# Opening of a hybrid encoder kernel: all 512 tokens taken channels-first, and the row norm applied to V, dt and K at their eviction

## The chip, the cores and the metric

The kernel runs on one core of a Trainium2 chip. The metric is the device time of one execution in microseconds (us); the kernel before is given as the median of three executions. Profiles are of one execution each, and positions such as "at 25.54" are microseconds from the start of its span.

## What is computed

One encoder layer on 512 tokens of 1024 channels. The part that the change touches is the first norm and the projections that read it:

```python
h = rmsnorm(x, pre_mix_norm[l])            # x * rsqrt(mean(x*x) + 1e-6) * g
proj = h @ w_in[l]                         # all projections in one matrix
z, xbc, dt_raw, q, k, v, gates = split_cols(proj, IN_SPLITS)
y_ssd  = ssd_branch(z, xbc, dt_raw, ...)   # bidirectional Mamba-2 scan
y_attn = window_attention(q, k, v, ...) @ w_attn_out[l]
...                                        # gates, output projection, norm, squared-ReLU MLP, norm
```

The norm's factor r = rsqrt(mean(x*x) + eps) is one number per token. A product of h with a weight may therefore be made from x*g without r, and r multiplied in afterwards.

## The kernel before, in words

**Arithmetic.** Nearly every product is made of three passes in the type fp32r: an operand a is split into a high part (a cast to fp32r, on ScalarE) and a low part (a minus the high part, on VectorE or GpSimd), and `mm3` (L456) adds high*high, high*low and low*high in PSUM. A product in plain fp32 needs no split, but shows in the trace as two matmul records, each slower per column.

**Quanta and order.** The program is a list of quanta, each a product with its weight chunks. A chunk is loaded into one of three raw buffers (`wr`), cast into `wh` by ScalarE and subtracted into `wl` by GpSimd in four pieces (L525, L529). Actions such as evictions are hung on a quantum number with `at`; a fraction such as 2.5 means the middle of quantum 2. After everything has been emitted, a planner (`Planner.plan`, called by `chain`, L549) orders the instructions of each engine by its own costs and fixes that order with dependencies. PSUM has eight banks: three of the tag `pp` (projections) and five of the tag `ps`, each handed out in a ring.

**The opening.** Eight warm-up products on a tile of ones (L682) come first. Then V (256 columns) and dt (64 columns) are made with tokens on the partitions, 320 columns at a time, contraction in eight pieces k of 128 channels:

- Tokens 0 to 255 arrive channels-first from the host (`in_xt`, tiles `xt`, five pieces `X_CHUNKS`). They are multiplied by the norm's gain g into `xg` (L697, L699), and the products `ps<-wr,xg` are plain fp32, 2 token blocks x 8 k (L643). r is put in at the eviction (L629, L630).
- All 512 tokens arrive a second time as token rows (`in_x`, tiles `x`, L715, eight loads of 256 KB), to get the mean squares (L723 on ScalarE, L724 on VectorE, L726 and L727 on GpSimd). For tokens 256 to 511 the rows are scaled by r (L760, L761), transposed on TensorE (L763, `tr` at L454, 16 of them) and split into `h` (L475, L476); their V and dt products are three-pass, 2 blocks x 8 k x 3 (L655).
- For tokens 0 to 255, r is spread over the partitions by `scale_tokens` (L730): a diagonal matrix `dg` times ones, in fp32, into a `pp` bank; `xg` times that gives `hf` (L743), which is split into the other half of `h` (L745, L746).
- `h` is complete before the first K product. The two K quanta (L896) follow, 24 matmuls of 512 columns each, and are split from PSUM straight into `KH` and `KL` (L888 to L891); then two Q quanta (L915, L916), the scores of attention head 0 (`ps<-KH,Q` and `ps<-KL,Q`), and the x quanta of the scan. `dt_math` (L813) computes dt and its running sums from the dt rows on the way.

## Time and profile before

| | |
|---|---|
| median of 3 executions | 1074.58 us (1074.38 to 1079.08) |
| the profiled execution's own time | 1074.73 us |
| its span in the profile | 1072.9 us |
| TensorE busy | 1062.9 us, 99% of the span |
| VectorE, ScalarE, GpSimd busy | 758.4, 656.8, 796.5 us |
| moved by DMA | 133.20 MB |

The profile's page lists, for each engine, busy time, the chain of work that ended last, and groups of equal instructions; a row of the timeline gives start, length, engine, line, operation, output<-inputs, shape and count, and in brackets how long the engine had been idle before and what released it. PE is TensorE's matmuls, PEld its weight loads, DVE VectorE, ACT ScalarE, POOL GpSimd, SP the queue that issues most loads. Lengths of matmul records overlap, so a pace is read from starts, not from lengths.

### The profile page before, as it was taken

Reading aid. Unit: us, or ns where it says so; the run is one execution under the profiler, and the core shown is the slowest. Engines: PE = TensorE matmul, PEld = TensorE weight load, DVE = VectorE, ACT = ScalarE, POOL = GpSimd, SP = SyncE. Lnnn points to the kernel's source line nnn. Section 1 sums busy time; section 2 is a strip of 40 time slices with the busy share of each in tenths; the row PEclk is TensorE's granted clock in tenths of the full one; section 3 lists DMA queues with packets and bytes.
Section 4 is the critical chain, followed back from the end, with each engine's and each line's share of the span. In section 5 each row is a group of like instructions: output and inputs, shape, how many; then the busy total and the mean of one; then the engine's idle time right before and its main releaser. Section 6 shows DMA issues by size and latency. Waiting matters only on the chain.

```text
span 1072.9 us, 16653 instructions
## 1 busy us (share of the span) xinstructions
PE 1062.9 (99%) x5542; PEld 894.7 (83%) x5542; DVE 758.4 (71%) x1363; ACT 656.8 (61%) x1409; POOL 796.5 (74%) x993
## 2 busy tenths in 40 slices
PE   9999999999999999999999999999999999999997
PEld 7888888888888888888888888889888888888885
DVE  5577778787885878787976536698663574574588
ACT  6766877676686867676777424466555444444552
POOL 5756458567677699899989966215587897898994
PEclk9999999999999999999999999999999999999999
DMA  8342324433443426244535544317211421424222
GB/s 287 117 129 89 123 79 121 146 102 103 130 119 108 154 99 182 87 136 142 165 109 153 177 150 145 112 59 262 89 68 67 152 97 60 157 93 150 73 99 78
DMA packets 61509, 133.20 MB, mean 124 GB/s; under 512 B 9064, under 2 KB 18920, under 8 KB 61424
## 3 DMA queue, kind: packets, MB, share of 16 engines
q1 hardware_dynamic: 61136, 131.76, 38.6%
q8 instruction: 43, 0.70, 0.3%
q10 hardware_dynamic: 288, 0.39, 0.1%
q14 instruction: 42, 0.34, 0.1%
HBM read 127.63 MB, written 4.49 MB: 123 GB/s over the span
## 4 chain that ended last, share of the span: by engine, by line
PE 97%; DVE 1%; DMA 1%; ACT 0%; issue 0%; POOL 0%; SPq 0%; DVEq 0%; POOLq 0%
PE pp L450 62%; PE ps L450 32%; PE ps L454 3%; DMA wr<-in_wv 1%; PE pp L454 0%; DVE x L1419 0%; DVE acc L1398 0%; SPq L690 0%; DVE wl L620 0%; DVEq L1783 0%; DVE ag L1698 0%; DVE h L1406 0%; POOLq L1783 0%; ACT wh L617 0%; POOL mrs L1412 0%
## 5 line engine op out<-in xcount | busy, mean ns | idle before, releaser
L529 POOL TENSOR_TENSOR wl<-wr,wh 128x256 fp32r<-128x256 f32 (+1 forms) x519 | 415.9, 831 | 166.5 <-ACT wh L525 163.2
L450 PE MATMUL pp<-h,wh 128*128 128x512 f32 (+1 forms) x1728 | 524.5, 385 | 0.0
L450 PEld LDWEIGHTS pp<-h,wh 128*128 128x128 f32 x1728 | 318.5, 188 | 61.6 <-issue 0.5
L450 PE MATMUL pp<-h,wl 128*128 128x512 f32 (+1 forms) x864 | 333.9, 386 | 0.0
L525 ACT CAST wh<-wr 128x1024 fp32r<-128x1024 f32 (+1 forms) x130 | 135.3, 1041 | 127.5 <-PE pp L450 99.4
L450 PEld LDWEIGHTS pp<-h,wl 128*128 128x128 f32 x864 | 162.4, 188 | 32.0 <-POOL wl L529 0.2
L1624 POOL TENSOR_TENSOR wl<-wd,wh 128x256 fp32r<-128x256 f32 x158 | 131.6, 871 | 11.8 <-ACT wh L1621 11.8
L1621 ACT CAST wh<-wd 128x512 fp32r<-128x512 f32 x92 | 53.2, 618 | 38.4 <-PE ps L450 21.6
L450 PE MATMUL ps<-wl,fh 128*128 128x512 f32 x184 | 71.7, 390 | 0.0
L450 PE MATMUL ps<-wh,fl 128*128 128x512 f32 x184 | 71.6, 389 | 0.0
L450 PE MATMUL ps<-wh,fh 128*128 128x512 f32 x184 | 71.6, 389 | 0.0
L1459 DVE SCALAR_TENSOR_TENSOR pp<-pp,r 128x256 f32<-128x256 f32 (+1 forms) x31 | 17.3, 559 | 65.5 <-ACT r L1456 65.4
L1183 ACT ACTIVATE n<-cb,tables 128x128 f32<-128x128 f32 x128 | 47.6, 392 | 16.0 <-DVE cb L1174 12.3
L1017 DVE SCALAR_TENSOR_TENSOR u<-pp,cv,u 128x510 f32<-128x510 f32 (+1 forms) x64 | 47.7, 746 | 10.1 <-ACT u L1013 8.8
L1222 POOL TENSOR_TENSOR w<-w,E 128x256 f32<-128x256 f32 x48 | 40.5, 858 | 16.2 <-DVE w L1218 15.2
L1184 ACT ACTIVATE m<-cb,tables 128x128 f32<-128x128 f32 x128 | 47.6, 390 | 7.2 <-DVE cb L1174 6.5
L1115 POOL TENSOR_TENSOR xd<-x,tables 128x256 f32<-128x256 f32 x48 | 32.4, 693 | 17.4 <-ACT x L1040 15.0
L1179 ACT ACTIVATE rf<-rf,tables 128x128 f32<-128x128 f32 x128 | 42.4, 392 | 4.1 <-DMA rf<-csT 4.1
L1177 POOL TENSOR_TENSOR rb<-rb,tables 128x512 f32<-128x512 f32 x32 | 36.6, 1147 | 9.9 <-DMA rb<-csT 7.9
L949 ACT ACTIVATE P<-P,mx 128x384 f32<-128x384 f32 (+1 forms) x64 | 35.2, 551 | 14.1 <-DVE mx L946 14.1
L1676 DVE TENSOR_TENSOR acc<-acc,ps 128x512 f32<-128x512 f32 x46 | 31.3, 680 | 15.8 <-PE ps L450 15.6
L1185 DVE TENSOR_TENSOR m<-m,n 128x512 f32<-128x512 f32 x32 | 29.5, 922 | 16.6 <-ACT m L1184 16.5
(291 smaller groups left out, 2202.7 us busy)
## 6 DMA issues: line engine op xcount, KB each, us to landing
wr<-in_w_in_b SPq DMA_DIRECT2D x74, 512.0 KB, 3.7
wr<-in_w_mlp_in_b SPq DMA_DIRECT2D x32, 512.0 KB, 3.5
wd<-in_w_mlp_out SPq DMA_DIRECT2D x64, 256.0 KB, 4.8
rb<-csT SPq DMA_DIRECT2D x32, 256.0 KB, 4.0
rf<-csT SPq DMA_DIRECT2D x32, 256.0 KB, 3.7
wr<-in_w_ssd_out_b SPq DMA_DIRECT2D x13, 512.0 KB, 3.4
x<-in_x SPq DMA_DIRECT2D x16, 256.0 KB, 4.7
E<-csE SPq DMA_DIRECT2D x32, 128.0 KB, 4.3
```

Source lines behind the costliest of these rows:

```text
L450: self.nc.tensor.matmul(out, lhsT, rhs, start=start, stop=stop, skip_group_check=more)
L525: self.nc.scalar.copy(hi[:, :m], raw)
L529: engines[e].tensor_tensor(lo[:, c], raw[:, c], hi[:, c].bitcast(F32), op=ALU.subtract)
L949: nc.scalar.activation(p[:, :w], p[:, :w], AF.Exp, bias=mx[:, n:n + 1], accum_out=sm[:, n:n + 1])
L1017: nc.vector.scalar_tensor_tensor(u[:, a:e], ps[:, a + d:e + d], self.wtap(t, b), u[:, a:e], op0=ALU.mult, op1=ALU.add)
L1177: nc.gpsimd.tensor_tensor(v4(rb), v4(rb), cs[:, 1].unsqueeze(2).to_broadcast([128, 4, 128]), op=ALU.subtract)
L1179: nc.scalar.activation(v4(rf)[:, h], v4(rf)[:, h], AF.Identity, bias=ncs[:, 0, h:h + 1])
L1183: nc.scalar.activation(v4(n)[:, h], cb[:, 0], AF.Copy, scale=dt[:, 0, h:h + 1])
L1184: nc.scalar.activation(v4(m)[:, h], cb[:, 1], AF.Copy, scale=dt[:, 1, h:h + 1])
L1222: nc.gpsimd.tensor_tensor(wc, wc, E[:, d], op=ALU.add)
L1621: nc.scalar.copy(hi, src)
L1624: (nc.vector if q == 512 else nc.gpsimd).tensor_tensor(lo[:, c], src[:, c], hi[:, c].bitcast(F32), op=ALU.subtract)
```

## The change

All eight channel pieces of all 512 tokens are now loaded channels-first, as eight tiles `xt` of 128x512; no token rows are loaded and nothing is transposed. Each `xt` is multiplied by g and split into a new pair `hr` ("raw h", without r) by ScalarE and VectorE. V, dt and K are made from `hr`: V and dt with four token blocks and three passes, except k = 0, which stays plain fp32 (`PLAIN = 1`); r is multiplied in when V and dt are evicted, and K is multiplied by r spread over the partitions (`rb`) when it is evicted, into a new tile `kf`, which is then split. The mean squares come from the `xt` tiles: ScalarE squares them, VectorE adds them into an even and an odd tile, and eight TensorE products with a single column of ones (`token_sums`) sum over the channels. One GpSimd power gives all four columns of r. `scale_tokens` now handles four token blocks, and makes `h` from `xt` for all 512 tokens, while K is already being computed. The planner's constants for early loads change too.

The core of the diff:

```diff
-X_CHUNKS = ((0, 1), (1, 3), (3, 5), (5, 7), (7, 8))
+W_CHUNKS = ((0, 1), (1, 2), (2, 5), (5, 8))
+PLAIN, SUMS_AT, SCALE_AT = 1, 2.5, 3.5
-RATE, EARLY, LAND = 260, 350, 2500
+RATE, EARLY, START, LAND = 260, 370, 20000, 2500
...
         def done(t, ps):
-            bias = self.row[:, :64]
-            if t < 2:
-                r = self.rst0[:, t:t + 1]
-                nc.scalar.activation(self.V[0][:, t], ps[:, :256], AF.Copy, scale=r)
-                nc.vector.scalar_tensor_tensor(self.dtv[:, t], ps[:, 256:320], r, bias, op0=ALU.mult, op1=ALU.add)
-            else:
-                nc.scalar.copy(self.V[1][:, t - 2], ps[:, :256])
-                nc.vector.tensor_tensor(self.dtv[:, t], ps[:, 256:320], bias, op=ALU.add)
...
+            bias, r = self.row[:, :64], self.rst0[:, t:t + 1]
+            nc.scalar.activation(self.V[t // 2][:, t % 2], ps[:, :256], AF.Copy, scale=r)
+            nc.vector.scalar_tensor_tensor(self.dtv[:, t], ps[:, 256:320], r, bias, op0=ALU.mult, op1=ALU.add)
...
+                for k in range(k0, k1):
+                    for t in range(4):
+                        ps = banks[t][:, :320]
+                        if k < PLAIN:
+                            self.mm(ps, self.xg[k][:, tok(t)], raw[:, k - k0], k == 0, k == 7)
+                        else:
+                            hi, lo = self.hr[k]
+                            self.mm3(ps, (hi[:, tok(t)], lo[:, tok(t)]), (wh[:, k - k0], wl[:, k - k0]), k == 0, k == 7)
...
+    def raw_tokens(self):
+        nc = self.nc
+        for k, x in enumerate(self.xt):
+            g = self.gT[:, k:k + 1]
...
+            hi, lo = self.hr[k]
+            self.split_by(hi, lo, x, g)
+        self.token_scales()
+
+    def token_scales(self):
...
+        even, odd = get("sq"), get("sq")
+        for k, x in enumerate(self.xt):
+            to = (even, odd)[k % 2]
+            if k < 2:
+                nc.scalar.activation(to, x, AF.Square, scale=D ** -0.5)
+            else:
+                sq = self.bank("pp")
+                nc.scalar.activation(sq, x, AF.Square, scale=D ** -0.5)
+                nc.vector.tensor_tensor(to, to, sq, op=ALU.add)
+        self.squares = even, odd
+
+    def token_sums(self, ones):
...
+        ps = self.bank("pp")
+        for t in range(4):
+            for sq in (even, odd):
+                self.mm(ps[:, t:t + 1], sq[:, t * 128:(t + 1) * 128], ones[:, :1], sq is even, sq is odd)
+        self.slots.put(even, odd)
+        nc.vector.tensor_scalar(self.rst0, ps[:, :4], EPS, None, op0=ALU.add)
+        nc.gpsimd.tensor_tensor(self.rst0, self.rst0, self.mhalf[:, 0:1].to_broadcast([128, 4]), op=ALU.pow)
...
         rb = self.bank("pp")
-        for t in range(2):
+        for t in range(4):
             dg = get("dg", (128, 128))
-            nc.gpsimd.tensor_scalar(dg, self.ident, self.rst0[:, t:t + 1], None, op0=ALU.mult)
+            nc.vector.tensor_scalar(dg, self.ident, self.rst0[:, t:t + 1], None, op0=ALU.mult)
             self.mm(rb[:, t * 128:(t + 1) * 128], ones, dg, True, True)
...
+        self.rb = get("rb")
+        nc.scalar.copy(self.rb, rb)
         for k in range(8):
-            x = hf[k // 2][:, k % 2 * 256:(k % 2 + 1) * 256]
-            nc.vector.tensor_tensor(x, rb[:, :256], self.xg[k], op=ALU.mult)
...
+            x = self.xt[k]
+            hi, lo = self.h[k]
+            nc.vector.scalar_tensor_tensor(x, x, self.gT[:, k:k + 1], rb, op0=ALU.mult, op1=ALU.mult)
             nc.scalar.copy(hi, x)
-            nc.gpsimd.tensor_tensor(lo, x, hi.bitcast(F32), op=ALU.subtract)
...
+            for e, c in ((nc.vector, slice(0, 512)),) if k % 2 else ((nc.gpsimd, slice(0, 256)), (nc.gpsimd, slice(256, 512))):
+                e.tensor_tensor(lo[:, c], x[:, c], hi[:, c].bitcast(F32), op=ALU.subtract)
...
         def k_done(ps):
+            x = get("kf")
+            nc.vector.tensor_tensor(x, ps, self.rb, op=ALU.mult)
...
-                nc.scalar.copy(KH[a], ps[a])
-                nc.vector.tensor_tensor(KL[a], ps[a], KH[a].bitcast(F32), op=ALU.subtract)
-                nc.scalar.copy(KH[b], ps[a])
+                nc.scalar.copy(KH[a], x[a])
+                nc.vector.tensor_tensor(KL[a], x[a], KH[a].bitcast(F32), op=ALU.subtract)
+                nc.scalar.copy(KH[b], x[a])
...
-        hh = lambda: self.h
+        hh = lambda: self.hr
         return [self.cm(self.d_w_in_b, C_K - 64 + 128 * i, hh, k_done) for i in range(2)]
```

What the planner makes of it, at three places. First TensorE, where the V and dt products end and K begins. Before, the last token block's last pass (bank ps_299, weights from k = 7) is followed at once by the first K matmul (pp_408):

```order
L450 MATMUL ps_299<-wh_170,h_105 128x320
L450 MATMUL ps_299<-wl_171,h_105 128x320
L450 MATMUL ps_299<-wh_170,h_106 128x320
L450 MATMUL pp_408<-h_91,wh_314 128x512
L450 MATMUL pp_408<-h_92,wh_314 128x512
```

Now the eight one-column sums stand between (pp_325; sq_188 is the even, sq_189 the odd tile of squares; one pair of the four is shown), and K (pp_382) reads `hr`:

```order
L452 MATMUL ps_213<-wh_161,hr_120 128x320
L452 MATMUL ps_213<-wl_162,hr_120 128x320
L452 MATMUL ps_213<-wh_161,hr_121 128x320
L452 MATMUL pp_325<-ones_79,sq_188 128x1
L452 MATMUL pp_325<-ones_79,sq_189 128x1
L452 MATMUL pp_382<-hr_106,wh_234 128x512
L452 MATMUL pp_382<-hr_107,wh_234 128x512
```

The two `dg` products that stood among the V products before have become four, and stand behind the first K quantum. Second, TensorE in the two Q quanta (pp_523 and pp_563), which are now the first to read `h`. Before, the quanta ran one after the other; now four matmuls of the second stand inside the first, ahead of the pass that needs h_101, the low part of k = 5:

```order
L452 MATMUL pp_523<-h_100,wh_372 128x512
L452 MATMUL pp_563<-h_90,wh_466 128x512
L452 MATMUL pp_563<-h_91,wh_466 128x512
L452 MATMUL pp_563<-h_90,wl_467 128x512
L452 MATMUL pp_563<-h_92,wh_466 128x512
L452 MATMUL pp_523<-h_101,wh_372 128x512
```

Third, VectorE from the spreading of r to the eviction of the second K quantum. Before, the queue of that stretch ran from the `hf` tiles (pp_261 is r spread out) through `dt_math` to the second K quantum's low parts (pp_454):

```order
L743 TENSOR_TENSOR hf_270<-pp_261,xg_115 128x256 x2
L743 TENSOR_TENSOR hf_271<-pp_261,xg_116 128x256 x2
L828 RECIPROCAL dtw_376<-dtw_376 128x256
L889 TENSOR_TENSOR KL_434<-pp_408,KH_433 64x512
L834 SCALAR_TENSOR_TENSOR dtw_377<-dtw_377,ps_379 128x256 x6
L889 TENSOR_TENSOR KL_480<-pp_454,KH_479 64x512
L889 TENSOR_TENSOR KL_486<-pp_454,KH_485 64x512
L916 SCALAR_TENSOR_TENSOR Q_527<-pp_502,Q_527 64x512
```

Now (pp_395 is r spread out, pp_382 and pp_473 the two K quanta; the rows of one kind are not all shown) the multiplication that empties the second K quantum's bank stands behind eight `h` tiles, four low parts, the whole of `dt_math`, a Q eviction and the first scores of head 0 (L928):

```order
L747 SCALAR_TENSOR_TENSOR xt_123<-xt_123,gT,pp_395 128x512
L868 TENSOR_TENSOR kf_450<-pp_382,rb_408 128x512
L750 TENSOR_TENSOR h_93<-xt_124,h_92 128x512
L747 SCALAR_TENSOR_TENSOR xt_130<-xt_130,gT,pp_395 128x512
L750 TENSOR_TENSOR h_105<-xt_130,h_104 128x512
L811 RECIPROCAL dtw_347<-dtw_347 128x256
L874 TENSOR_TENSOR KL_453<-kf_450,KH_452 64x512
L817 SCALAR_TENSOR_TENSOR dtw_348<-dtw_348,ps_350 128x256 x6
L904 SCALAR_TENSOR_TENSOR Q_548<-pp_523,Q_548 64x512
L821 SCALAR_TENSOR_TENSOR dtw_349<-tables_344,row 128x256
L928 ISA P_614,mx_608<-ps_611,bt_521,row 128x256
L868 TENSOR_TENSOR kf_498<-pp_473,rb_408 128x512
```

What moved: K's eviction has become a step of VectorE that needs r, and it comes later in that queue; the bank it empties is the one that the first x quantum of the scan takes next. From the second x quantum of the scan on, some 280 matmuls into the program, TensorE's order is the same in both kernels.

More of the change, by code (lines that the diff above doesn't have):

```diff
@@ L666, in start @@
+        return [product(*c) for c in V_CHUNKS]
     def start(self):
@@ L709, in start @@
-        self.at(1, lambda: self.scale_tokens(ones, xg))
+        self.at(1, lambda: self.bcast_row(self.row, self.d_row, 176))
+        self.at(SUMS_AT, lambda: self.token_sums(ones))
+        self.at(SCALE_AT, lambda: self.scale_tokens(ones))
         self.at(1, self.later_constants)
-    def load_tokens(self, t):
-        xs = [self.slots.get("x") for _ in range(2)]
-        for j, x in enumerate(xs):
-            self.nc.sync.dma_start(x, self.d_x[0, t * 128:(t + 1) * 128, j * 512:(j + 1) * 512])
-        return xs
@@ L732, in scale_tokens @@
+    def scale_tokens(self, ones):
         nc = self.nc
```

143 lines of the change are left out of this document (49 added, 94 removed).

## The prediction

> **What bounds the kernel now.** I read the busy times first, then the chain of work that ended last, then what TensorE waited for.
>
> ```profile
> PE 1062.9 (99%) x5542; PEld 894.7 (83%) x5542; DVE 758.4 (71%) x1363; ACT 656.8 (61%) x1409; POOL 796.5 (74%) x993
> PE 97%; DVE 1%; DMA 1%; ACT 0%; issue 0%; POOL 0%; SPq 0%; DVEq 0%; POOLq 0%
> PE pp L450 <- DVE two L675: 1.0, 1, 1.0
> PE ps L450 <- ACT xg L697: 0.6, 1, 0.6
> PE ps L450 <- DMA wr<-in_wv: 0.3, 1, 0.3
> PE ps L450 <- ACT h L475: 0.2, 1, 0.2
> PE pp L454 <- ACT x L760: 0.2, 1, 0.2
> ```
>
> TensorE is busy 99% of the span, and it is 97% of the chain that ended last. The five waits are all that it has in the whole program, and all of them lie in the opening. So the change is worth what it does to TensorE's work and idle time before the scan begins. Behind that, TensorE's order of matmuls is the same in both kernels; what is gained or lost at the start is carried to the end unchanged, as long as nothing becomes late there.
>
> **The opening, in paces.** The timeline of TensorE (start, length, records; length of a group includes the drain of its last):
>
> ```profile
> 4.61 2.81 PE L450 MATMUL ps<-wr,xg 128*128 128x320 f32 x8
> 9.04 6.19 PE L450 MATMUL ps<-wr,xg 128*128 128x320 f32 x22 [0.57 <-ACT xg L697]
> 15.69 0.38 PE L454 MATMUL ps<-ident,x 128*128 128x128 f32 x2
> 15.90 0.38 PE L454 MATMUL pp<-ident,x 128*128 128x128 f32 x2
> 21.43 0.46 PE L450 MATMUL ps<-wh,h 128*128 128x320 f32 x2
> 21.87 0.46 PE L450 MATMUL ps<-wh,h 128*128 128x320 f32 x2
> 22.90 0.56 PEld L450 LDWEIGHTS pp<-dg,ones 128*128 128x128 f32 x4
> 23.38 0.19 PEld L450 LDWEIGHTS ps<-wl,h 128*128 128x128 f32 x1
> 25.54 0.63 PE L450 MATMUL pp<-h,wh 128*128 128x512 f32 x2
> 26.23 0.62 PE L450 MATMUL pp<-h,wh 128*128 128x512 f32 x2
> ```
>
> A plain fp32 product of 320 columns is two records; 22 records in 6.19 us make 0.55 us each product. Three fp32r passes of 320 columns start 21.87 - 21.43 = 0.44 apart, so 0.147 each. Two transposes take 0.21, so about 0.11 each. Two `dg` products (four records) hold the weight loader for 23.38 - 22.90 = 0.48, so 0.24 each. Three passes of 512 columns take 26.23 - 25.54 = 0.69, so 0.23 each and 5.45 for a quantum of 24. The first K matmul stands at 25.54. Between 4.61 and there lie 16 x 0.55 + 48 x 0.147 + 16 x 0.11 + 2 x 0.24 = 18.1 us of work in 20.9 us: **2.8 us are idle or slow**, and that is all that a better-fed opening could win beside a change of the work itself.
>
> **The work.** Taken away: 12 plain products (6.6) and 16 transposes (1.8). Added: 36 fp32r passes (5.3), two `dg` products (0.5), and eight one-column sums. No such matmul stands in the trace. Each loads 128x128 fp32 weights like `dg`, but streams 1 column instead of 128: from above 8 x 0.24 = 1.9, from below nothing. I take 1.9, since the weight loads are the part of the `dg` row that stays the same. The net is -0.7 us (-2.6 if the sums are free).
>
> The Trainium skill ("TensorE: Matmul & The Clock Gate", section "LDWEIGHTS (loading the stationary operand)") says that a load takes as long as its 128 weight columns need at 1.2 GHz, 107 ns, whatever is streamed behind it. By it, my estimate for sixteen loads would be 1.7 us, and the sum below 0.2 lower; the 0.12 us per load of the `dg` row agrees with it as far as it goes.
>
> **When the data are there.** Loads, by two-microsecond stretches (last figure GB/s), and a chunk of weights that ScalarE waited for:
>
> ```profile
> 2.00:4.00 2.00, 2.00 (x12) 2.00 (x11) 0.00 (x0) 1.12 (x2) 0.00 (x0) 1.00 0.95 297
> 4.00:6.00 2.00, 2.00 (x8) 1.57 (x8) 1.47 (x4) 1.23 (x2) 0.99 (x1) 1.00 1.09 317
> 6.00:8.00 2.00, 1.71 (x7) 0.96 (x6) 0.33 (x1) 0.41 (x1) 0.18 (x1) 1.00 0.98 354
> 8.00:10.00 2.00, 1.43 (x6) 0.72 (x5) 1.74 (x4) 1.39 (x3) 1.17 (x1) 1.00 1.03 396
> 10.00:12.00 2.00, 2.00 (x9) 1.45 (x8) 1.22 (x3) 1.87 (x4) 0.80 (x1) 1.00 1.05 399
> 10.13 0.99 ACT L617 CAST wh<-wr 128x960 fp32r<-128x960 f32 x1 [0.74 <-DMA wr<-in_wv]
> ```
>
> By 10.0 us 2.7 MB have moved. The last V weights, with all that was issued ahead of them, are 2.3 MB, moved by 8.8; they were usable at 10.1, so 1.3 later. In the new order of SP's queue the weights of k = 2 to 4 complete 1.68 MB (moved 7.2, usable 8.5) and the last `xt` 3.48 MB (moved 11.8, usable 13.1). The token rows, 2 MB, are gone from the queue and 1 MB of `xt` is new, so the later weight chunks come no later.
>
> **ScalarE in the opening.** Prices:
>
> ```profile
> L617 ACT CAST wh<-wr 128x640 fp32r<-128x640 f32 x1 | 0.7, 725 | 1.1 <-DMA wr<-in_wv 1.1
> L723 ACT ACTIVATE junk<-x 128x512 f32<-128x512 f32 x4 | 2.5, 622 | 1.0 <-DMA x<-in_x 1.0
> L760 ACT ACTIVATE x<-x,rst 128x512 f32<-128x512 f32 x2 | 1.4, 722 | 0.2 <-POOL rst L727 0.2
> L525 ACT CAST wh<-wr 128x1024 fp32r<-128x1024 f32 x8 | 8.4, 1052 | 0.7 <-PE ps L450 0.6
> ```
>
> Eight squares (0.62), eight scaled casts (0.72), seven casts of 320 columns (0.46, from 640 taking 0.725 and 960 taking 0.99), one weight cast for K (1.05) and two small ones (0.6) are 15.6 us in ScalarE's queue, from 4.2, when the first `xt` is there. Less an overlap of some 0.06 at each of 26 seams and with short waits for loads, the last square ends near 19.9, VectorE's addition near 20.6. TensorE meanwhile: the four plain products from 4.7, as slow at first as the eight records above (2.81), to 7.2 or so; k = 1 to 9.0; a gap to 9.55, until ScalarE has cast the weights of k = 2 behind two squares; then six k of 12 passes, 72 x 0.147 = 10.6, to 20.1. Its wait for the squares is 0.5, the sums 1.9, a return to fp32r 0.1: **K starts near 22.6, 2.9 earlier.** Four `dg` products now follow the first K quantum (0.96), so the Q quanta start 28.0 + 1.0 + 5.5 = 34.5 instead of 25.54 + 10.9 = 36.4: **1.9 earlier.**
>
> **The wait that is added.** r now ends in a GpSimd power of four columns, behind seven `wl` pieces:
>
> ```profile
> L529 POOL TENSOR_TENSOR wl<-wr,wh 128x256 fp32r<-128x256 f32 x32 | 22.7, 744 | 11.5 <-ACT wh L525 11.5
> L727 POOL TENSOR_TENSOR rst<-rst,mhalf 128x1 f32<-128x1 f32 x4 | 2.6, 660 | 0.3
> ```
>
> 7 x 0.74 from 18.4 with the wait for the second cast at 21.0 puts the power at 24.2 to 25.2 (one column takes 0.66; I allow 1). The `dg` tiles are ready by 26.3 and TensorE wants them at 28.0: hidden, with 1.7 in hand. The V evictions behind it hold four `ps` banks till 27, and the next `ps` product is the scores, far later: nothing.
>
> **The queue behind r** is the place that can cost. From 29.0, when r stands spread in PSUM, VectorE works through the third excerpt above the prediction, up to the eviction of K's second bank:
>
> ```profile
> L1329 DVE SCALAR_TENSOR_TENSOR ps<-gate,ps 128x512 f32<-128x512 f32 x5 | 3.5, 693 | 15.5 <-PE ps L450 15.5
> L1624 DVE TENSOR_TENSOR tl<-wd,th 128x512 fp32r<-128x512 f32 x17 | 11.7, 713 | 0.3
> L468 DVE TENSOR_TENSOR fl<-ft,fh 128x512 fp32r<-128x512 f32 x20 | 19.3, 967 | 3.6 <-ACT fh L467 3.6
> L828 DVE RECIPROCAL dtw<-dtw 128x256 f32<-128x256 f32 x1 | 1.8, 1753 | 1.6 <-ACT dtw L827 1.6
> L834 DVE SCALAR_TENSOR_TENSOR dtw<-dtw,ps 128x256 f32<-128x256 f32 x7 | 2.9, 418 | 0.2
> ```
>
> Eight `h` tiles at 0.69 less overlap (5.1), two K multiplications (1.3), five subtractions with both inputs in SBUF at 0.71 to 0.97 (I take 0.95: 4.7), the reciprocal (1.75), eleven steps of `dt_math` at 0.42 (4.6), a Q eviction (0.7) and a score (0.6) are 18.8 us: K's second bank is free at about 47.9. TensorE gets to it after K (34.5), two Q quanta (45.4), the scores and the sums of `dt_math`:
>
> ```profile
> 47.32 0.28 PE L450 MATMUL ps<-KH,Q 128*128 128x256 f32 x1
> 48.49 0.63 PE L450 MATMUL pp<-h,wh 128*128 128x512 f32 x2
> 52.39 1.04 PE L450 MATMUL ps<-dtw,cst 128*128 128x128 f32 x6
> ```
>
> The scores are 48.49 - 47.32 = 1.2, the `dt_math` sums about 0.9, so 47.5. The wait there is 0.4 by this, up to 2.5 if ScalarE's casts come late too; nothing if the subtractions run at 0.71. I charge 0.7, and 0.3 for `h` pieces in the Q quanta, where the planner already put four matmuls of the second into the first.
>
> **Sum.** The profiled execution took 1074.73 (span 1072.9 and 1.83 around it), 0.15 above the median. 1074.73 - 1.9 + 1.0 = **1073.8 us**.
>
> **Rivals.** (1) *The sums are nearly free and VectorE keeps up*: -1.9 - 1.5 = -3.4, **1071.3**. For it: only one column streams. Against: the same weights are loaded.
>
> (2) *VectorE's queue holds the scan's first bank.* The Q and scan quanta wait for VectorE, whose subtractions wait for GpSimd's `wl` pieces, which run one behind the other there. The rows speak for it: 0.97 with two SBUF inputs beside GpSimd against 0.69 with one in PSUM. If each of the five waits a whole piece (0.74), and the `h` casts on ScalarE come late as well, the wait grows by 3 to 4 and the time is **1077.3**, slower than before. It decides once the bank comes more than 2.3 after TensorE's turn; for 0.5% it would have to be 7.
>
> The Trainium skill ("SBUF — State Buffer", section "Who interferes with whom") says that such an instruction and a GpSimd one that reads SBUF exclude each other for a whole instruction. By it (2) is no accident, but its length hangs on which starts first; the 0.97 above agrees.
>
> (3) *The change does not feed the opening better*: ScalarE's queue, not the loads, ends the V products. If its overlap is nil and the loads come 1 us later, K starts at 24.1 and the time is **1075.3**. Against: TensorE needs 20.1 by its own passes.
>
> **Chances.** The forecast 0.58, (1) 0.14, (2) 0.18 and (3) 0.10. About 0.5% (5.4 us) is what a measurement of this kernel can tell from no change, and hardly any of these reaches it: only the far end of (2), or an effect of the new order later in the program, where VectorE and ScalarE stand a little differently: 0.08 slower; 0.04 faster, since 2.8 idle and 2.6 of work is the most there is; 0.88 the same. The range takes in (1) and most of (2): 1071.0 to 1077.5.
>
> **What would show it.** Right: the first K matmul near 22.6, the sums 1.5 to 1.9 long, ScalarE without gaps from 9 to 20, the first x matmul about 48.5 and a wait for `kf` of 0 to 1 ahead of it. Wrong: sums under 0.5, a K start past 24, TensorE waiting for VectorE by more than 2 before the scan, or new waits behind it.

## The result, and the profile after

| | before | changed |
|---|---|---|
| median | 1074.55 us (20 runs) | 1076.38 us (20 runs) |
| ratio to before | | 1.0019, 95% interval [1.0011, 1.0026] |
| the profiled execution's own time | 1074.73 us | 1076.19 us |
| its span | 1072.9 us | 1074.1 us |

The changed kernel is 1.8 us slower. The interval does not contain 1, so the slowdown is clear of the noise, though it is well inside the 0.5% of the chances. The forecast was 0.9 us faster. 1076.38 lies within the stated range, but on the other side of the time before.

First the busy times and the chain that ended last, from the changed kernel's page:

```profile
PE 1062.2 (99%) x5558; PEld 895.8 (83%) x5558; DVE 771.1 (72%) x1367; ACT 660.3 (61%) x1408; POOL 791.2 (74%) x984
PE 93%; DVE 3%; ACT 1%; issue 1%; DMA 1%; SPq 0%; POOL 0%; DVEq 0%; POOLq 0%; ACTq 0%
```

TensorE's busy time fell by 0.7 us (1062.9 to 1062.2), the net that the prediction had for its work. But its share of the chain fell from 97% to 93%, and VectorE's rose from 1% to 3%: somewhere VectorE now decides. Where, the waits of TensorE tell:

```profile
PE ps L452 <- ACT pT L954: 1.4, 1, 1.4
...
PE pp L452 <- POOL h L750: 1.0, 1, 1.0
PE ps L452 <- DVE dtw L821: 0.4, 1, 0.4
```

The old opening's waits for loads, `h` and `x` (0.7 us together) are gone, and that for `xg` is down from 0.6 to 0.2. Three new ones have come: 1.0 us for a scaled tile `h`, 0.4 for the step sizes `dtw`, and 1.4 for `pT`, which belongs to attention head 1 and which no step of the change touches.

TensorE's timeline gives the marks of the prediction (start, length, records, and in brackets the idle time ahead; the last row is VectorE's):

```profile
20.15 1.84 PE L452 MATMUL pp<-ones,sq 128*128 128x1 f32 x16
21.85 0.71 PE L452 MATMUL pp<-hr,wh 128*128 128x512 f32 x2
27.42 1.05 PE L452 MATMUL pp<-dg,ones 128*128 128x128 f32 x8
28.23 0.71 PE L452 MATMUL pp<-hr,wh 128*128 128x512 f32 x2
33.79 0.61 PE L452 MATMUL pp<-h,wh 128*128 128x512 f32 x2
37.87 0.50 PE L452 MATMUL pp<-h,wh 128*128 128x512 f32 x1 [0.97 <-POOL h L750]
47.75 1.15 PE L452 MATMUL ps<-dtw,cst 128*128 128x128 f32 x6 [0.40 <-DVE dtw L821]
48.76 0.73 PE L452 MATMUL pp<-h,wh 128*128 128x512 f32 x2
...
48.02 0.69 DVE L868 TENSOR_TENSOR kf<-pp,rb 128x512 f32<-128x512 f32 x1
```

In this pair of traces the opening is better than forecast: K starts at 21.85 (before 25.54), the Q quanta at 33.79. To see what is left of that I set the matmuls of the two traces side by side, one by one, by tile names and shape. At 61 us the changed kernel is 0.64 us ahead, at 77.9 still 0.51; at the second pair of head 2's scores it is 1.08 us behind, and it stays 1.1 behind to the last matmul, 990 us later. **So in this pair the whole loss is one step of 1.6 us at 78 to 79 us.** The rest of the difference of the profiled executions (0.26) lies outside the spans. (In the mean of all runs 2.01 us of the changed kernel's time lie outside the span, and 1.84 of the time before; why is not known.)

One pair is not enough for the opening, though. Nine of the kernels profiled here, this one included, have the changed opening, and three the old one. In the nine, K starts at 21.79 to 22.82, 22.2 on average; in the three at 24.57, 25.15 and 25.54, 25.1 on average. So K starts 2.9 us earlier on average, as forecast, and 3.69 in this pair, whose trace of before is the latest of its three. The lead of 0.64 at 61 us is therefore this pair's; between the averages it would be about nothing. The step at 78 us lies between two places of the same traces and does not hang on this.

That place, in the kernel before (timeline, TensorE, then ScalarE, then VectorE):

```profile
76.69 1.26 PE L454 MATMUL ps<-ident,P 128*128 128x128 f32 x10
78.06 0.44 PE L450 MATMUL ps<-KH,Q 128*128 128x384 f32 x1
...
77.54 0.73 ACT L966 COPY pT<-ps 128x256 f32<-128x256 f32 x2
...
77.44 0.97 DVE L966 COPY pT<-ps 128x384 f32<-128x384 f32 x2
```

and in the changed one:

```profile
76.19 1.25 PE L456 MATMUL ps<-ident,P 128*128 128x128 f32 x10
79.13 0.44 PE L452 MATMUL ps<-KH,Q 128*128 128x384 f32 x1 [1.45 <-ACT pT L954]
...
75.95 0.63 ACT L1011 ACTIVATE th<-u 128x512 f32<-128x512 f32 x1 [1.69 <-DVE u L1005]
76.49 1.04 ACT L527 CAST wh<-wr 128x1024 fp32r<-128x1024 f32 x1
77.56 0.59 ACT L903 ACTIVATE Q<-pp 64x512 fp32r<-64x512 f32 x1
78.17 0.51 ACT L1033 ACTIVATE w<-u,dcol 128x256 f32<-128x256 f32 x1
78.71 0.75 ACT L954 COPY pT<-ps 128x256 f32<-128x256 f32 x2
...
78.18 0.69 DVE L904 SCALAR_TENSOR_TENSOR Q<-pp,Q 64x512 fp32r<-64x512 f32 x1 [0.85 <-ACT Q L903]
78.90 0.89 DVE L954 COPY pT<-ps 128x384 f32<-128x384 f32 x2
```

TensorE turns head 1's probabilities in ten products (`ps<-ident,P`) that fill four `ps` banks; two copies on ScalarE and two on VectorE (`pT`) empty them, and head 2's scores go into banks of the same ring. Before, the copies start 0.8 us after the products and the scores find a bank at once. Changed, the products come 0.5 us earlier, but the copies 1.2 to 1.5 later: on ScalarE they stand in the fixed order behind `th`, a weight cast, a Q eviction and `w`; `th` waits 1.69 for VectorE's `u`; and VectorE's two stand behind a Q subtraction that waits for ScalarE's Q. Before, ScalarE's copies also stood behind `th`, a Q eviction and three more, and started 2.5 us after `th` (75.05); now it is 2.8 after `th`, and `th` is 0.9 later. **Theory A** is therefore: VectorE is late, the fixed orders hand its lateness to the copies, and the copies hold TensorE.

Why is VectorE late? Its busy time from 36 to 62 us (last line of the table by stretches; before, then changed):

```profile
sum 26.00, PE 26.00 PEld 21.95 DVE 17.29 ACT 17.01 POOL 14.86; mean PE 13.00 PEld 10.98 DVE 8.64 ACT 8.51 POOL 7.43
```

```profile
sum 26.00, PE 24.63 PEld 19.95 DVE 23.79 ACT 18.35 POOL 14.32; mean PE 12.31 PEld 9.97 DVE 11.89 ACT 9.18 POOL 7.16
```

17.3 us of 26 before, 23.8 now. In the changed kernel r comes once for all tokens, at 24 us, so everything that hangs on it stands behind it in one queue: the scaling of the tiles, low parts, K's evictions, the step sizes. From 39.2 to 62.4 us VectorE does not idle. It is also more work: up to 80 us VectorE's busy time rises from 50.7 to 61.1 us, while GpSimd's falls from 48.7 to 44.6. The diagonal tiles (2.85) were GpSimd's before, and the low parts of every other scaled tile (3.0) in part. No run tells the added work from the late r.

Rivals: **(B)** the copies' order alone makes them late, whatever VectorE does; **(C)** the waits at 37.9 and 47.8 each cost their length at the end as well, as the prediction added them up.

### The profile page after: what moved, and what is told of

The parts are those of the page before. It is cut to its first block, busy times and chain, and to the rows that moved or that the text cites. A ratio compares the mean times of both kernels' runs of the same rounds, so it can differ in the third digit from the quotient of the medians.

```text
span 1074.1 us, 16670 instructions
## 1 busy us (share of the span) xinstructions
PE 1062.2 (99%) x5558; PEld 895.8 (83%) x5558; DVE 771.1 (72%) x1367; ACT 660.3 (61%) x1408; POOL 791.2 (74%) x984
## 4 chain that ended last, share of the span: by engine, by line
PE 93%; DVE 3%; ACT 1%; issue 1%; DMA 1%; SPq 0%; POOL 0%; DVEq 0%; POOLq 0%; ACTq 0%
PE pp L452 59%; PE ps L452 32%; PE ps L456 3%; DMA wr<-in_wv 1%; DVE u L1005 1%; DVE P L928 0%; DVE KL L874 0%; ACT wh L527 0%; DVE dtw L817 0%; DVE Q L904 0%; DVE P L943 0%; ACT h L748 0%; DVE x L1407 0%; DVE acc L1386 0%; ACT P L937 0%
## 5 line engine op out<-in xcount | busy, mean ns | idle before, releaser
L452 PE MATMUL pp<-h,wh 128*128 128x512 f32 (+1 forms) x1696 | 515.2, 385 | 1.0 <-POOL h L750 1.0
L452 PEld LDWEIGHTS pp<-h,wh 128*128 128x128 f32 x1696 | 312.5, 188 | 62.0 <-POOL h L750 1.4
L452 PE MATMUL pp<-h,wl 128*128 128x512 f32 (+1 forms) x848 | 327.4, 386 | 0.0
L452 PEld LDWEIGHTS pp<-h,wl 128*128 128x128 f32 x848 | 159.4, 188 | 31.3 <-issue 0.2
L1447 DVE SCALAR_TENSOR_TENSOR pp<-pp,r 128x256 f32<-128x256 f32 (+1 forms) x31 | 17.3, 559 | 65.3 <-ACT r L1444 65.2
L1005 DVE SCALAR_TENSOR_TENSOR u<-pp,cv,u 128x510 f32<-128x510 f32 (+1 forms) x64 | 47.8, 746 | 10.2 <-ACT u L1001 8.9
L452 PEld LDWEIGHTS ps<-wl,fh 128*128 128x128 f32 x184 | 34.5, 188 | 7.5 <-POOL wl L1612 0.3
```

The source lines that it names most:

```text
L452: self.nc.tensor.matmul(out, lhsT, rhs, start=start, stop=stop, skip_group_check=more)
L1005: nc.vector.scalar_tensor_tensor(u[:, a:e], ps[:, a + d:e + d], self.wtap(t, b), u[:, a:e], op0=ALU.mult, op1=ALU.add)
```

## The experiments

Most of these kernels differ from the changed one (two: from the one before) only in the planned order of one or two engines, the others in a width or in the sums as well (in two of these the planner is made to price the altered step as before, or at nothing, so that its other orders stay). `orders[e]` is the planned order of engine e, `made(e, name)` lists its instructions that write a tile of that name, `move` puts some of them ahead of another. The medians of before that were taken beside them are 1074.56 and 1074.44, so theirs may be set beside 1076.38.

### The copies first

```diff
+pt = made("ACT", "pT_")[2:4]
+move("ACT", pt, [n for n in made("ACT", "wh_") if n in orders["ACT"][:orders["ACT"].index(pt[0])]][-1])
+pt = made("DVE", "pT_")[2:4]
+move("DVE", pt, [n for n in made("DVE", "Q_") if n in orders["DVE"][:orders["DVE"].index(pt[0])]][-1])
```

> One change of order in the changed kernel, every engine else as it was: the copies of head 1's turned scores out of the two ps banks go ahead of work that needs no bank. On ScalarE the two stand ahead of a weight cast, a Q eviction and a w; on VectorE ahead of one Q subtraction. Theory A (TensorE loses 1.5 us before head 2's scores because these copies stand behind other work in their engines' fixed orders, and the loss is carried to the end): the wait of 1.45 us on pT falls under 0.3, the order behind it hides the later cast, and the time is 1.2 to 1.6 us under the changed kernel's, near 1074.8, about the time before. Rival B (the copies are late because what they read or what is ahead of them is late anyway, and the order costs little): the wait stays over 1.0 and the time is within 0.4 us of the changed kernel's. Rival C (the wait goes, but the delayed cast, Q or w makes a new one): a wait on wh, Q or w of about 1 us within the next 10 us, time within 0.5 us of the changed kernel's.

Measured 1075.12 us, ratio to before 1.0003 [0.9995, 1.0012]: 1.26 under the changed kernel's. TensorE's and ScalarE's timeline there:

```profile
78.47 0.34 PE L452 MATMUL ps<-KH,Q 128*128 128x384 f32 x1
...
77.56 0.37 ACT L967 COPY pT<-ps 128x256 f32<-128x256 f32 x1
```

The second pair of scores has no bracket any more: the wait is gone, and no new one has come behind it. The offset to the changed kernel steps by 1.6 us (0.96 to -0.66) at just this matmul. The place of the copies is what TensorE pays at 79 us. It is not all of the 1.83: by the medians 0.56 over before is left, and the part on why the prediction was wrong says where it went.

### The Q quantum's wait

```diff
+lo = made("POOL", "h_")
+wl = [n for n in made("POOL", "wl_") if orders["POOL"].index(lo[3]) < orders["POOL"].index(n) < orders["POOL"].index(lo[4])]
+move("POOL", lo[4:6], wl[0])
```

> One change of order on GpSimd alone in the changed kernel: the low part of the scaled tile that the Q quantum waits 0.97 us for goes ahead of a low part of a weight that is needed 10 us later. Theory A (VectorE, without idle from 39.2 to 62 us, decides when TensorE may go on at 47.8 and 48.8; the Q quantum's wait lies under that): the wait at 37.9 us falls under 0.2, the wait for the step sizes' dtw at 47.8 grows from 0.40 to about 1.3, and the time stays within 0.3 us of the changed kernel's, 1076.2. Rival B (each wait of TensorE adds to the end): the wait goes, none grows, and the time is 0.8 to 1.0 us less, 1075.3.

> The two changes of order of the other kernels in one: the turned scores' copies first on ScalarE and VectorE, and on GpSimd the scaled tile's low part ahead of the weight's. Theory A (only the late copies cost at the end; the Q quantum's wait is hidden under VectorE's): the time of the first of the two alone, near 1074.8, within 0.3 us. Rival B (the waits add): 0.9 us below that, near 1073.8.

Measured 1076.65 (ratio to before 1.0018 [1.001, 1.0027]) alone, and 1075.01 (1.0009 [1.0, 1.0018]) with the copies first. So moving this piece gains nothing at the end: theory A on the time. TensorE, of the kernel with this edit alone:

```profile
37.45 0.50 PE L452 MATMUL pp<-h,wh 128*128 128x512 f32 x1 [0.19 <-POOL h L762]
40.44 0.50 PE L452 MATMUL pp<-h,wh 128*128 128x512 f32 x1 [0.43 <-POOL h L762]
48.23 1.15 PE L452 MATMUL ps<-dtw,cst 128*128 128x128 f32 x6 [0.40 <-DVE dtw L833]
```

The way there was another than expected. The wait for `dtw` did not grow; instead GpSimd's next low parts came late, 0.43 at 40.4, and the gain was gone before Q ended (12.25 us from the first Q matmul to the first score, 12.14 in the changed kernel). So the run took the wait at 37.9 away, but not the lateness of Q, and does not decide (C) for this wait. GpSimd's queue as a whole sets the Q quanta, not the one piece, and behind it `dtw` sets the sums.

### VectorE relieved

```diff
-nc.vector.scalar_tensor_tensor(p, p, 1.0 / n, s2, op0=ALU.add, op1=ALU.mult)
+nc.vector.scalar_tensor_tensor(p[:, 0], p[:, 0], 1.0 / n, s2[:, 0], op0=ALU.add, op1=ALU.mult)
```

> Seven VectorE steps of the step sizes' series run on 64 columns instead of 256 (the series is left out for three of the four token tiles); every engine's order is that of the changed kernel. At 0.42 us for 256 columns, and an estimated 0.2 for 64, VectorE is relieved by 1.5 us at 42.5 to 46.3 us and of nothing elsewhere. Theory A (the copies of head 1's turned scores are late because VectorE is over a microsecond behind from 47 us on, and ScalarE's silu input waits for it): the wait for dtw at 47.8 goes (0.4), x starts about 0.6 earlier, the convolution of the first x quantum ends at about 60.2 instead of 61.6, and of the wait of 1.45 before head 2's scores over half goes; time 0.8 to 1.8 us under the changed kernel's, near 1074.9. Rival B (the copies are late by their engines' order whatever VectorE's backlog): only the 0.4 goes, and is lost again at the same place; time within 0.4 us of the changed kernel's.

Measured 1074.91, ratio to before 1.0003 [0.9995, 1.0012]: 1.5 under the changed kernel's, from seven short instructions 31 us and more ahead of the place. (VectorE, TensorE:)

```profile
42.43 1.48 DVE L819 SCALAR_TENSOR_TENSOR dtw<-dtw,ps 128x64 f32<-128x64 f32 x6
...
77.64 0.44 PE L454 MATMUL ps<-KH,Q 128*128 128x384 f32 x1 [0.88 <-ACT pT L956]
```

Six steps take 1.48 instead of 2.68, `th` comes 1.47 earlier (74.48), and the wait for `dtw` is gone. Against (B), as far as it says "whatever VectorE does"; what the orders would cost by themselves is not shown. But the wait for `pT` shrank only to 0.88: TensorE itself came 0.9 earlier to that place, since x starts as soon as `dtw` and K's last eviction allow. So the half of (C) that is about the wait at 47.8 holds: what VectorE gains there, TensorE gains. A relief of VectorE is earned twice, once ahead of x and once at the copies, and the two shares add to the 1.5.

### VectorE's idle time filled

At 37.2 us the changed VectorE waits 1.27 for ScalarE's high part of the last tile, with the reciprocal of the step sizes, whose input is there since 30.3, behind it in its order.

```diff
+dt, ps = made("DVE", "dtw_")[4], made("DVE", "ps_")[0]
+move("DVE", [dt, ps], made("DVE", "h_")[3])
```

> One change of order on VectorE alone in the changed kernel: the reciprocal of the step sizes and the product behind it go ahead of the last low part of a scaled tile, for which VectorE waits 1.27 us (37.2 to 38.5 us) while the reciprocal's input has been there since 30.3. Theory A (VectorE's lateness from 39 us on is what TensorE pays for, first at the step sizes' sums, then at the copies of head 1's turned scores): the wait of 1.27 us is filled, the sums' wait of 0.40 goes, the convolution of the first x quantum ends about 1 us earlier than 61.6, and the time is 0.5 to 1.3 us under the changed kernel's, near 1075.3; the low part that now comes later may cost the last Q pair up to 0.5. Rival B (ScalarE's order alone makes the copies late): within 0.3 us of the changed kernel's.

> Both changes of order, the reciprocal early and the copies of the turned scores first, with all work kept. Theory A (VectorE's lateness and the copies' place each cost at the end): the copies' place gives 1.3 to 1.6 us as it did alone, the reciprocal another 0.4 to 0.9, together 1073.8 to 1074.5, at or under the time before (1074.56). Rival B (with the copies first nothing more depends on VectorE before 79 us): the time of the copies alone, 1075.1 within 0.3 us.

Measured 1075.11 (1.0004 [0.9995, 1.0013]) for the reciprocal alone, and **1073.60** (0.9992 [0.9983, 1.0001]) with the copies first as well. The first one's VectorE and TensorE:

```profile
38.13 1.74 DVE L822 RECIPROCAL dtw<-dtw 128x256 f32<-128x256 f32 x1
...
78.64 0.45 PE L452 MATMUL ps<-KH,Q 128*128 128x384 f32 x1 [0.86 <-ACT pT L965]
```

No wait stands ahead of the reciprocal any more, and the one for `pT` is again 0.86. With both edits the list of TensorE's waits, beside the one for the first constants at the very start, comes down to one:

```profile
...
PE pp L452 <- POOL h L765: 1.0, 1, 1.0
```

That version keeps all work, is 2.8 us under the changed kernel and 1.0 under the one before by the medians; nine of its eleven runs lie under the lowest of the 27 of before (1073.99), though the interval still includes 1. That it comes within 0.2 of the forecast's 1073.8 is partly luck: it has a relief of VectorE that the forecast did not have (x comes 0.88 earlier by it). With the copies alone repaired the time is 1075.12.

### The fault made in the kernel before

```diff
+pt = made("ACT", "pT_")[2:4]
+behind = [n for n in made("ACT", "Q_") if n in orders["ACT"][orders["ACT"].index(pt[1]):]][0]
+move("ACT", [behind], pt[0])
```

> The kernel before, with one change of order on ScalarE: a Q eviction of 0.59 us that stands behind the copies of head 1's turned scores goes ahead of them. It is the changed kernel's fault made in a small dose in the kernel that lacks it. Theory A (these copies free the ps banks just as head 2's scores need them, with no slack): the second pair of head 2's scores, at 78.06 without a wait, comes 0.5 to 0.7 us later (more if that Q's product itself is not ready), with a wait on pT, and the offset is carried to the end: 1075.1 to 1075.3. Rival B (the copies have slack in the kernel before, so that another thing makes the wait in the changed one): no wait on pT, within 0.2 us of the time before.

Measured 1074.33, ratio 1.0001 [0.9992, 1.0009]: nothing. TensorE, ScalarE, VectorE:

```profile
77.09 0.45 PE L450 MATMUL ps<-KH,Q 128*128 128x384 f32 x1
...
77.32 0.76 ACT L978 COPY pT<-ps 128x256 f32<-128x256 f32 x2
...
76.48 0.97 DVE L978 COPY pT<-ps 128x384 f32<-128x384 f32 x2
```

The scores go on before ScalarE's copies have begun. So the second and third pairs (77.09 and 77.55) must have got the banks that VectorE empties, from 76.48 on; that banks go out in the planned order of their release is inferred from this. The expectation had overlooked that four banks from two engines make a ring: one late engine is not enough in this dose. So both were delayed, VectorE's by the Q subtraction that waits for that Q:

```diff
+pt = made("DVE", "pT_")[2:4]
+behind = [n for n in made("DVE", "Q_") if orders["DVE"].index(n) > orders["DVE"].index(pt[1])][0]
+move("DVE", [behind], pt[0])
```

> The kernel before; on ScalarE a Q eviction (0.59 us) ahead of its two copies of head 1's turned scores, and on VectorE the Q subtraction that waits for that eviction (0.69 us) ahead of its two, so that neither engine frees a ps bank early (the run that delayed ScalarE alone left VectorE's two early, and lost nothing). Theory A (head 2's scores need the banks just when the copies free them): the second pair of head 2's scores, or the third, waits 0.4 to 1.0 us on pT, TensorE's offset against the kernel before steps up by that much there and stays to the end; time 0.4 to 1.0 us over the time before. Rival B (the copies have over a microsecond of slack there, and the changed kernel's wait has another cause): no wait on pT and no step.

```profile
78.32 0.44 PE L450 MATMUL ps<-KH,Q 128*128 128x384 f32 x1 [0.52 <-ACT pT L981]
...
77.89 0.75 ACT L981 COPY pT<-ps 128x256 f32<-128x256 f32 x2
...
78.62 0.89 DVE L981 COPY pT<-ps 128x384 f32<-128x384 f32 x2
```

Measured 1075.26, ratio 1.0007 [0.9998, 1.0016]: 0.8 over before. The offset to before steps by 0.65 at this matmul, by 0.87 within a microsecond, and holds to 616 us. (The profiled execution is longer than the median, 1079.66, for a wait of 2.6 us for `yl` at 617 us, far from the edit, and a clock of 0.51 for 3.4 us behind it.) The wait of the changed kernel is made here without any part of the change, at a third of its length (0.52), and the interval just includes 1.

### Only ScalarE's copies first

> The changed kernel with only ScalarE's two copies of the turned scores put first; VectorE's two stay behind its Q subtraction, at 78.9 us. Theory A (the four banks come from both engines, so the last late pair decides): the second and third pair of head 2's scores go without a wait, the fourth waits 0.8 to 1.6 us on VectorE's copy, and the time is 0 to 0.6 us under the changed kernel's. Rival B (ScalarE's copies alone were the fault, as the profile's releaser says): the wait goes, and the time is that of both moved, 1075.1 within 0.3 us.

(The edit is the first two lines of the first diff.) Measured **1077.73**, ratio to before 1.0039 [1.0024, 1.0053]: not faster but 1.35 slower than the changed kernel. TensorE, VectorE:

```profile
80.76 0.38 PE L452 MATMUL ps<-KH,Q 128*128 128x256 f32 x1 [2.26 <-DVE pT L965]
...
79.42 0.69 DVE L915 SCALAR_TENSOR_TENSOR Q<-pp,Q 64x512 fp32r<-64x512 f32 x1 [2.04 <-ACT Q L914]
80.14 0.89 DVE L965 COPY pT<-ps 128x384 f32<-128x384 f32 x2
```

As theory A had it, the second and third pairs go without a wait and the fourth waits for VectorE: the releaser that the profile named in the changed kernel (ScalarE) was only the first of two late ones. But the price was misjudged. ScalarE's Q now stands behind its copies, and VectorE's copies wait for that Q: 2.26 us, not 0.8 to 1.6. And in the profiled execution the granted clock fell behind the wait (stretch, its length, busy times; the figure behind POOL's is the clock). That execution took 1083.27, 5.5 over the median; a wait of 2.6 for `yl` at 623 us, again with a slow clock behind it, is most of the rest.

```profile
80.70:82.70 2.00, 1.94 (x7) 1.67 (x8) 1.97 (x9) 0.00 (x0) 0.95 (x2) 0.72 0.09 12
82.70:84.00 1.30, 1.30 (x4) 1.01 (x4) 0.51 (x3) 0.72 (x3) 0.00 (x0) 0.50 0.83 211
```

### The sums, twice

```diff
-            for sq in (even, odd):
-                self.mm(ps[:, t:t + 1], sq[:, t * 128:(t + 1) * 128], ones[:, :1], sq is even, sq is odd)
+            for _ in range(2):
+                for sq in (even, odd):
+                    self.mm(ps[:, t:t + 1], sq[:, t * 128:(t + 1) * 128], ones[:, :1], sq is even, sq is odd)
```

> The eight one-column sums are issued twice (the second set writes the same values), nothing else moved. Theory A (TensorE's opening up to K is a chain through the sums, the scale, the diagonal products and the scaled tiles, so that a delay there goes to the end in full): K starts 1.7 us later (eight more at 0.21 us), every mark up to 79 us moves by 1.6 to 1.8, and the time is 1.5 to 1.9 us over the changed kernel's, near 1078.0. Rival B (TensorE's waits at 37.9, 47.8 and 79.1 us take part of it up): 0.3 to 1.0 us over, 1076.7 to 1077.4, with those waits shorter. Rival C (a one-column product costs TensorE next to nothing behind its neighbour): K at the same time, and within 0.3 us.

Measured 1079.97, ratio to before 1.005 [1.0037, 1.0063]: 3.6 over the changed kernel, twice what any theory gave. TensorE's timeline:

```profile
20.49 3.63 PE L452 MATMUL pp<-ones,sq 128*128 128x1 f32 x32
23.98 1.07 PE L452 MATMUL pp<-hr,wh 128*128 128x512 f32 x2
25.28 1.05 PE L452 MATMUL pp<-hr,wh 128*128 128x512 f32 x2
```

and its table by stretches (the clock is the figure behind POOL's):

```profile
20.00:24.00 4.00, 4.00 (x38) 4.00 (x36) 0.01 (x1) 1.05 (x1) 2.73 (x4) 1.00 0.45 132
24.00:26.00 2.00, 2.00 (x7) 1.62 (x7) 0.69 (x2) 0.53 (x2) 1.60 (x2) 0.53 0.00 0
26.00:28.00 2.00, 2.00 (x7) 1.53 (x7) 2.00 (x4) 1.04 (x3) 2.00 (x4) 0.61 0.33 80
```

The products are priced as measured above: 32 records in 23.98 - 20.49 = 3.49, so 0.109 a record. The K passes behind them take (25.28 - 23.98) / 3 = 0.43 instead of 0.23, and the clock there is 0.53 and 0.61. The eight passes up to 27.4 lose 1.6 us, the extra products 1.75: together 3.4 of the 3.6. Rivals B and C fall, and theory A had the path right and the price wrong, since it left the clock out: a delay ahead of K goes to the end in full, since the scale, the diagonal products and the scaled tiles all hang on it.

### The second set elsewhere

> The changed kernel with a second set of eight one-column sums into columns that nothing reads, put 5.5 us behind the first set, between K's products and the diagonal ones. The run that issued both sets back to back lost 3.6 us: 1.75 for the products themselves, and the rest where the granted clock fell to 0.53 and 0.61 behind 3.5 us of one-column products. Theory A (the clock falls only behind an unbroken stretch of such products longer than the 1.7 us of one set): the granted clock stays at 1.00, the diagonal products and all behind them come 1.7 to 1.8 us later, and the time is 1.5 to 1.9 us over the changed kernel's, near 1078.1. Rival B (any second set costs the clock): 3 us or more over, with a clock under 0.8 somewhere from 27 to 33 us. Rival C (behind K the waits at 37.9 and 47.8 take it up): under 1.2 us over.

Measured 1083.10, ratio to before 1.0081 [1.0068, 1.0093], 6.7 over the changed kernel: the run did not test what it was for. The second set stood at 27.36 there. TensorE, VectorE, and two stretches with the clock behind POOL's figure:

```profile
31.44 2.77 PE L452 MATMUL pp<-dg,ones 128*128 128x128 f32 x8 [2.24 <-DVE dg L756]
...
29.24 0.16 DVE L746 TENSOR_SCALAR rst<-pp 128x4 f32<-128x4 f32 x1 [9.21 <-PE pp L452]
...
31.00:34.00 3.00, 2.56 (x9) 2.08 (x9) 3.00 (x8) 2.07 (x5) 3.00 (x6) 0.50 0.52 173
34.00:36.00 2.00, 2.00 (x6) 1.61 (x6) 1.04 (x3) 1.83 (x6) 2.00 (x4) 0.50 0.56 90
```

The second set went into other columns of the same bank, and the scale `rst` waited for it as well, 7.2 us later than in the changed kernel (22.03). So TensorE stood idle for 2.24 right behind the second set, and the clock was 0.50 up to 36 us. By the letter both signs of rival B came (over 3 us, and a clock under 0.8), but the wait may be as much to blame as the sums. The Q quanta start 6.8 later than in the changed kernel: 1.7 for the sums, 2.2 for the wait, and 2.9 for the clock (eight `dg` records take 2.43 instead of 0.81, and six K passes behind them 0.44 each instead of 0.23). Whether the clock would have stayed up with dense work on both sides stays open.

### Fewer sums

The three edits of order that move the copies and the reciprocal, and beside them:

```diff
-            for sq in (even, odd):
-                self.mm(ps[:, t:t + 1], sq[:, t * 128:(t + 1) * 128], ones[:, :1], sq is even, sq is odd)
+            self.mm(ps[:, t:t + 1], even[:, t * 128:(t + 1) * 128], ones[:, :1], True, True)
...
+        nc.vector.tensor_tensor(even, even, odd, op=ALU.add)
...
+        pw = made("POOL", "rst0")[:1]
+        wl = [n for n in made("POOL", "wl_") if orders["POOL"].index(n) < orders["POOL"].index(pw[0])][-2:]
+        move("POOL", pw, wl[0])
```

> All work kept: the copies of the turned scores first, the reciprocal early, and at the opening the two sums of squares added on VectorE, so that four one-column products do instead of eight, with the square root's pow ahead of two low parts of weights on GpSimd. Theory A (a chain through the sums, the scale, the diagonal products and the scaled tiles sets what follows): K starts 0.85 us earlier (four at 0.21 fewer) and all marks to 79 us move by 0.6 to 0.9; time 0.6 to 0.9 under the version with the two changes of order, near 1072.8, 1.7 us under the time before. Rival B (the added sum on VectorE, 0.97 us, is late for the sums, or the two low parts are late for K): K starts no earlier or waits, within 0.3 us of 1073.6.

Measured 1074.04, ratio to before 0.9998 [0.9989, 1.0007]; its runs (1073.29 to 1076.84) overlap those of the version without this edit. K started at 21.45, 0.4 earlier than in the changed kernel's trace, with a wait of 0.36 of the sums for the added squares, which took 1.21 rather than 0.97. (In the trace of the version without this edit K starts at 22.31, 0.86 later; by the spread of the openings neither figure can be taken for the edit's.) At 79 us its matmuls stand 2.87 us ahead of the changed kernel's, the version without it 2.03; at the end 2.45 and 2.09. A gain of 0.58 was given back near 593 us, at a wait for `m`. The time can't be told from 1073.60.

## Why the prediction was wrong, step by step

- **TensorE's work, -0.7**: right (1062.9 to 1062.2 us of busy time). The eight sums, sixteen records, took 1.70 (20.15 to 21.85) against 1.9 charged. The Trainium skill ("TensorE: Matmul & The Clock Gate", section "LDWEIGHTS (loading the stationary operand)") gives 107 ns a load, by which the estimate was 1.7; the trace agrees, with 0.106 a record.
- **K start 22.6, Q quanta 34.5**: right. 21.85 and 33.79 in the changed kernel's trace, but 22.2 for K on average, 2.9 before the average of before, as forecast. No wait stood ahead of the sums (0.5 charged), and four `dg` products took 0.81 (0.96 charged).
- **The power hidden**: right. It ended at 24.05, in front of products that TensorE reached at 27.42.
- **0.3 for `h` in the Q quanta**: too small, 0.97 there, and 1.2 over all of Q. That it cost nothing at the end is argued, not shown: x could not start before K's second bank was free at 48.71, and the GpSimd piece moved did not shorten Q.
- **VectorE's queue behind r**: the right wait, priced too low. K's second bank came free at 48.71 (48.02 and 0.69), forecast 47.9; counted from K's first matmul that is 26.9 us against 25.3. The scaling of the tiles began at 29.31, 1.1 after TensorE had left the `dg` products (28.23), where nothing was charged, and VectorE waited 1.27 for ScalarE inside the queue. TensorE's wait of 0.40 was for `dtw`, which stands just ahead in that queue. That x stood at 48.76 nevertheless (forecast 48.5) is luck: K was early in that execution. From K's start to 61 us the changed kernel gave up 3.05 of its lead (3.69 to 0.64), where 2.0 was charged (2.9 to 0.9).
- **The step that failed** is the one put as a premise: "what is gained or lost at the start is carried to the end unchanged, as long as nothing becomes late there". TensorE's order is indeed the same there, but something became late. VectorE's queue was followed to the bank that x needs, and dropped at that point, when it had no idle time for another 14 us. What was late at 48 was handed to and fro between VectorE and ScalarE up to 76 us, reached `th` 0.9 later than before, and met a planned order in which four bank-freeing copies stand behind work that was not urgent. That cost 1.6: TensorE's lead of 0.51 became 1.1 behind, 1.2 by the spans, and with 0.26 outside them the 1.46 between the profiled executions. Put together from the averages over these traces and runs: 0.9 faster forecast, 1.05 more given up between K and 61 us, 1.6 at the copies and 0.17 outside the spans make 1.9 slower; the medians say 1.83.
- **The rivals**: the second one was near, VectorE's backlog with the price on the slower side, but had it at the scan's first bank at 48 us, where the wait was 0.4. "New waits behind it" was named as a sign of being wrong, and is the one that came. That the measured time lies in the range is owed to the room made for this rival, not to a mechanism that the prediction had for the copies.

Shown: the copies' place (moving them takes the wait away; making both pairs late in the kernel before makes it), and VectorE's backlog as its feed (two different reliefs far ahead of it each take 0.6 of the wait's 1.45, and bring TensorE to the place 0.8 to 0.9 earlier). Only argued: that r's coming once, at 24 us, is what piled VectorE's work up, and not the work that was added to it; no run undid either part.

## What to carry to other kernels

Where a bound engine's order stays the same, that does not carry a gain to the end: follow each queue that the change loads until it idles again, and look at what that engine, or one that waits for it, must free in that stretch. Where several engines empty one ring of banks, the releaser that the profile names speaks for one matmul and one bank; before moving its copies, look at the others', because freeing one alone can make the next wait longer. In a fixed order, the cheap repair is to put what frees a bank ahead of what nobody waits for, and to fill a wait with an instruction whose inputs have long been there. And a lead at the opening that is read from one pair of traces is worth no more than the openings agree among themselves, here 1.0 us.

## What the runs showed of the hardware

The granted clock was 1.00 behind 1.70 us of one-column products and behind waits of 1.36 to 1.45 us. It fell to 0.53 behind 3.49 us of one-column products, during which the profile shows TensorE busy 4.00 of 4.00, to 0.50 behind 1.7 us of them followed at once by a wait of 2.24, and to 0.50 behind a wait of 2.26 us. So in these runs such products did not hold the clock up, and a busy PE column does not show it. That they are plain fp32 is not the reason: products of 320 columns in that type ran at 1.00 in the kernel before, from 10 to 12 us.

The Trainium skill ("TensorE: Matmul & The Clock Gate", section "What's actually happening") says that the clock halves after one idle window of about 3.4 us in a count that runs freely, and comes back after a busy one. The length of the slow stretch agrees (23.98 to 27.4 us, 3.4); a wait of 2.26 was already enough in the run above. In that run's profiled execution the matmuls behind the wait lost 1.6 us to the clock on top of the 0.8 of the longer wait, 2.4 together, where the medians differ by 1.35: the price differs from execution to execution. (The mean granted clock was 0.996 in the profiled execution and 0.999 in the median one.)
